# Attention scores over 64 rows: matmuls of the two row halves issued next to each other, in differential attention and in MLA

## The chip, the cores and the metric

One core of one Trainium2 chip runs the whole program, two transformer blocks of two layers each on 256 tokens of width 1024, in one launch. The metric is the device time of a launch in microseconds; a kernel's time is the median of its runs. Three runs of the kernel before gave 1356.26, 1359.81 and 1360.58 us.

## The reference

What is computed, cut to the two attentions that the change touches. Everything is float32.

```python
# first block, both layers: differential attention, 4 heads of two components of 64 each
s = jnp.einsum('bqhcd,bkhcd->bhcqk', qblk, k)      # c: component, contraction over 64
pr = jax.nn.softmax(s, axis=-1)
a = pr[:, :, 0] - lam * pr[:, :, 1]
o = jnp.einsum('bhqk,bkhe->bqhe', a, v)

# second block, layer 1: MLA, 8 heads; 128 "nope" dimensions and 64 with rotary positions
q = jnp.concatenate([q[..., :128], rope(q[..., 128:], positions)], axis=-1)
k = jnp.concatenate([k[..., :128], rope(k[..., 128:], positions)], axis=-1)
sc = jnp.einsum('bqhd,bkhd->bhqk', qi, k) * 192 ** -0.5     # causal mask on sc
o = jnp.einsum('bhqk,bkhd->bqhd', jax.nn.softmax(sc, axis=-1), v)
```

Around them stand a long convolution, a pooling mixer, projections and, in each of the four layers, a mixture of experts, whose weights make up nearly all of the 397 MB that the kernel reads.

## The kernel before

Weights come from HBM in tiles of 1 MB through one queue of SyncE (line 566). They land in a ring of 22 slots that they share with most intermediate tiles (`s8`); a transfer is issued when a slot is free, and a few tiles ahead of use. A projection splits each weight into a high and a low part (ScalarE line 593, VectorE line 595) and runs three matmuls per product. All matmuls are recorded at line 603 (`mm`) and all transposes by TensorE at line 616, so they are told apart by their tiles. A float32 matmul of `mm` shows as two MATMUL instructions with a weight load each; the bfloat16 mask shows as one.

The kernel is written against a tile framework. The source gives the order in which the instructions are made; when the program is built, a scheduler lays down each engine's queue, taking an instruction up when its operands and its buffer should be ready and preferring the one that comes earlier in the source. Each engine then works through its queue. PSUM has four banks under the name `pa` (`self.ps()`) and four under `pp` (`self.pp()`); a bank is given out again when its last reader is done.

**Differential attention** (`DiffAttention.scores`, line 319 on; called by `mix1` for two tiles of 128 queries, `qt`, and two pairs of heads, `hp`). `qkT` holds component 0 of a head in partitions 0 to 63 and component 1 in partitions 64 to 127. One call makes four score matmuls with a contraction over 64 rows, each 256 columns wide: two heads `z` of component `c` = 0 into bank `sc[0]`, then two of `c` = 1 into `sc[1]`. Behind each component come one row maximum (line 330) and two exponentials (line 333). `mix1` calls scores(0, 0) and scores(0, 1), then the projection of the values, and then interleaves `values`, scores(1, 0) and scores(1, 1); the output projection follows.

**MLA** (`mla`, with the inner functions `scores` and `values`). A call of `scores(hp)` handles two heads of one parity, heads 4·quad + par and 4·quad + par + 2, for both tiles `t` of 128 queries; keys run to (t + 1)·128. Per tile and head it makes three matmuls into one bank per tile: the causal mask (`identb`, `causb`), the nope part over 128 rows (`qnT`, `knT`), and the rope part over 64 rows (`qrT`, `krT`, both cut from the tile `RT`). Two heads of the same parity have their rope rows in the same half of the partitions. Then, per tile: one row maximum for both heads (line 1843), a multiply with the query scale (line 1844), two exponentials (line 1847), a reciprocal (line 1848) and two scalings (line 1850). `values(hp)` transposes the probabilities (tile `LX`), copies them (line 1863) and multiplies with `vv`. The order in the source is scores(0), scores(1), the projection of the values (`vup`), then values(0), scores(2), values(1), scores(3), values(2), values(3), and the attention to the memory (tiles `kv`, `MQ`).

Of the kernel before, what the change touches and what calls it, by code (L numbers as in the profile page):

```python
# [16 lines left out]
AF = mybir.ActivationFunctionType  # L17
OP = mybir.AluOpType
AX = mybir.AxisListType.X
# [274 lines left out]
def a2(a):  # L294
    return a.rearrange("p (a b) -> p a b", a=2)
# [6 lines left out]
def a8(a):  # L302
    return a.rearrange("p (a b) -> p a b", a=8)
# [6 lines left out]
class DiffAttention:  # L310
# [9 lines left out]
    def scores(self, qt, hp):  # L320
        k, nc, v = self.k, self.k.nc, self.k.nc.vector
        qs = slice(qt * 128, (qt + 1) * 128)
        sc = [k.ps(), k.ps()]
        ex, sm, cf = self.EX[:, hp], self.sm[qt], self.cf[qt]
        nm = k.sb([128, 2, 2], "anm", bufs=4)
        for c in range(2):
            for z in range(2):
                h = 2 * hp + z
                k.mm(sc[c][:, z * 256:(z + 1) * 256], self.qkT[c * 64:(c + 1) * 64, 0, h, qs], self.qkT[c * 64:(c + 1) * 64, 1, h, :], z == 0)
            v.tensor_reduce(nm[:, c, :], a2(sc[c]), axis=AX, op=OP.max, negate=True)  # L330
            for z in range(2):
                h = 2 * hp + z
                nc.scalar.activation(ex[:, z, c, :], sc[c][:, z * 256:(z + 1) * 256], AF.Exp, bias=nm[:, c, z:z + 1], accum_out=sm[:, c, h:h + 1])
        hs = slice(2 * hp, 2 * hp + 2)
        v.reciprocal(cf[:, 0, hs], sm[:, 1, hs])
        v.scalar_tensor_tensor(cf[:, 0, hs], cf[:, 0, hs], self.nlam, sm[:, 0, hs], op0=OP.mult, op1=OP.mult)
        for z in range(2):
            h = 2 * hp + z
            v.scalar_tensor_tensor(ex[:, z, 0, :], ex[:, z, 1, :], cf[:, 0, h:h + 1], ex[:, z, 0, :], op0=OP.mult, op1=OP.add)
# [130 lines left out]
class Kern:  # L470
# [1251 lines left out]
    def mla(self, hT, cat, row):  # L1722
        nc, v = self.nc, self.nc.vector
# [26 lines left out]
        knT = self.s8([128, 8, 256], "knT")  # L1750
        RT = self.s8([128, 2, 4, 256], "RT")
        qrT, krT = RT[:, 0], RT[:, 1]
# [27 lines left out]
        qs = self.sb([128, 3, 2, 8], "qss")  # L1780
        qnT = self.s8([128, 8, 256], "qnT")
# [23 lines left out]
        for t in range(2):  # L1805
# [3 lines left out]
            x, y = a8(pp[t]), a8(qx)  # L1809
            self.rotate((y[:, :, 0:32], y[:, :, 32:64]), (x[:, :, 0:32], x[:, :, 32:64]), [tq[:, t, j, :] for j in range(4)], [128, 8, 32])  # L1810
            p = self.ps()
# [5 lines left out]
        for t in range(2):  # L1817
# [3 lines left out]
            p = self.ps()  # L1821
# [5 lines left out]
        LX = self.s8([128, 2, 1024], "LX")  # L1827
        ex = {}

        def scores(hp):  # L1830
            par, quad = hp % 2, hp // 2
            for t in range(2):
                w = (t + 1) * 128
                ts = slice(t * 128, (t + 1) * 128)
                p = self.ps()
                for z in range(2):
                    h = 4 * quad + par + 2 * z
                    self.mm(p[:, z * w + t * 128:(z + 1) * w], self.identb, self.causb, z == 0)
                    self.mm(p[:, z * w:(z + 1) * w], qnT[:, h, ts], knT[:, h, 0:w], False)
                    self.mm(p[:, z * w:(z + 1) * w], qrT[par * 64:(par + 1) * 64, h // 2, ts], krT[par * 64:(par + 1) * 64, h // 2, 0:w], False)  # L1840
                r = qs[:, 2, t, 4 * quad + par:4 * quad + par + 3:2]
                nm = self.sb([128, 3, 2], "lnm", bufs=4)
                v.tensor_reduce(nm[:, 0, :], a2(p[:, :2 * w]), axis=AX, op=OP.max, negate=True)
                v.tensor_mul(nm[:, 0, :], nm[:, 0, :], r)
                e = a2(LX[:, hp % 2, t * 256:t * 256 + 2 * w])
                for z in range(2):
                    nc.scalar.activation(e[:, z, :], p[:, z * w:(z + 1) * w], AF.Exp, bias=nm[:, 0, z:z + 1], scale=r[:, z:z + 1], accum_out=nm[:, 1, z:z + 1])
                v.reciprocal(nm[:, 2, :], nm[:, 1, :])
                for z in range(2):
                    v.tensor_scalar(e[:, z, :], e[:, z, :], nm[:, 2, z:z + 1], None, op0=OP.mult)  # L1850
                ex[hp, t] = e

        def values(hp):
            par, quad = hp % 2, hp // 2
            po = self.pp()
            for z in range(2):
                h = 4 * quad + par + 2 * z
                pt = self.ps()
                self.transp(pt[:, 0:128], ex[hp, 0][:, z, :])
                self.transp(pt[:, 128:256], ex[hp, 1][:, z, 0:128])  # L1860
                self.transp(pt[:, 256:384], ex[hp, 1][:, z, 128:256])
                pT = self.tmp(384)
                nc.scalar.activation(pT, pt[:, 0:384], AF.Copy)
                self.mm(po[:, z * 256:(z + 1) * 256], vv[:, 0, h * 128:(h + 1) * 128], pT[:, 0:256], z == 0)
                self.mm(po[:, z * 256 + 128:(z + 1) * 256], vv[:, 1, h * 128:(h + 1) * 128], pT[:, 256:384], False)
            self.split(a2(po), cat.t[quad][0][:, par::2, :], cat.t[quad][1][:, par::2, :])

        scores(0)
        scores(1)
        for n in range(2):  # L1870
            pz = up2("vup", n)
            for t in range(2):
                nc.scalar.activation(vv[:, t, n * 512:(n + 1) * 512], pz[t], AF.Copy)
        for hp in range(4):
            values(hp)
            if hp < 2:
                scores(hp + 2)
# [192 lines left out]
```

## Time and profile before

| what | value |
|---|---|
| median of the three runs | 1359.81 us |
| the profiled execution's own time | 1360.22 us |
| its span, first to last instruction | 1358.6 us |
| TensorE matmul busy (PE) | 1233.9 us, 91% |
| weight load (PEld), VectorE (DVE), ScalarE (ACT) busy | 755.3, 644.7, 485.0 us |
| GpSimd (POOL) busy | 48.9 us |
| mean granted TensorE clock | 0.963 |
| read from HBM | 395.74 MB, 292 GB/s over the span |

All times below are microseconds from the start of the span. Matmuls are pipelined: their recorded durations overlap, so the cost of one is read from the distance between starts. PE counts as busy from the first start to the modelled end of such a row; a change in what the engine needs between two matmuls shows as distance, not always as idle time.

### The profile page before, as it was taken

Reading aid. Unit: us, or ns where it says so; the run is one execution under the profiler, and the core shown is the slowest. Engines: PE = TensorE matmul, PEld = TensorE weight load, DVE = VectorE, ACT = ScalarE, POOL = GpSimd, SP = SyncE. Lnnn points to the kernel's source line nnn. Section 1 sums busy time; section 2 is a strip of 40 time slices with the busy share of each in tenths; the row PEclk is TensorE's granted clock in tenths of the full one; section 3 lists DMA queues with packets and bytes.
Section 4 is the critical chain, followed back from the end, with each engine's and each line's share of the span. In section 5 each row is a group of like instructions: output and inputs, shape, how many; then the busy total and the mean of one; then the engine's idle time right before and its main releaser. Section 6 shows DMA issues by size and latency. Waiting matters only on the chain. (4 is left out here: it accounts for less than half of the span.)

```text
span 1358.6 us, 18043 instructions
## 1 busy us (share of the span) xinstructions
PE 1233.9 (91%) x6632; PEld 755.3 (56%) x6632; DVE 644.7 (47%) x1820; ACT 485.0 (36%) x991; POOL 48.9 (4%) x61
## 2 busy tenths in 40 slices
PE   6999999998999999998999888786899998977877
PEld 5777754456877764445888432231498676313222
DVE  6867853327868971216776410110387656101011
ACT  4456532224565642114665210010357653100001
POOL 1300000000200000000011000000000101000000
PEclk9999989998999999998999899899899998989989
DMA  9455568994154558997073899999960537999997
GB/s 373 182 220 208 186 259 344 422 415 184 66 217 178 228 216 368 400 402 308 29 278 145 326 408 421 421 421 422 393 246 31 223 119 301 422 421 421 421 422 253
DMA packets 68434, 398.07 MB, mean 293 GB/s; under 512 B 7408, under 2 KB 17904, under 8 KB 23024
## 3 DMA queue, kind: packets, MB, share of 16 engines
q1 hardware_dynamic: 68336, 396.82, 73.0%
q8 instruction: 55, 0.90, 0.3%
q14 instruction: 43, 0.35, 0.1%
HBM read 395.74 MB, written 1.05 MB: 292 GB/s over the span
## 5 line engine op out<-in xcount | busy, mean ns | idle before, releaser
L603 PE MATMUL pa<-w,xg 128*32 128x512 f32 (+1 forms) x1536 | 293.5, 651 | 52.8 <-DMA w<-in_w 52.2
L603 PEld LDWEIGHTS pa<-w,xg 128*32 128x32 f32 (+1 forms) x1536 | 78.6, 127 | 240.8 <-issue 137.0
L595 DVE TENSOR_TENSOR wlo<-w,whi 128x512 fp32r<-128x512 f32 (+1 forms) x260 | 178.3, 697 | 46.9 <-PE pp L603 36.6
L593 ACT ACTIVATE whi<-w 128x512 fp32r<-128x512 f32 (+1 forms) x260 | 158.0, 628 | 112.2 <-PE pp L603 93.5
L603 PE MATMUL pa<-w,tmp 128*32 128x512 f32 (+2 forms) x832 | 170.2, 575 | 13.3 <-DMA w<-in_w 13.1
L1321 DVE SCALAR_TENSOR_TENSOR tmp<-tmp,rgs,pa 128x256 f32<-128x256 f32 x32 | 15.4, 481 | 316.9 <-ACT tmp L1320 316.6
L613 DVE TENSOR_TENSOR wlo<-pa,whi 128x512 fp32r<-128x512 f32 (+1 forms) x68 | 44.9, 660 | 188.7 <-ACT whi L612 188.7
L603 PEld LDWEIGHTS pa<-w,tmp 128*32 128x32 f32 (+1 forms) x832 | 43.1, 119 | 100.9 <-issue 66.4
L612 ACT ACTIVATE whi<-pa 128x512 fp32r<-128x512 f32 (+1 forms) x68 | 38.9, 572 | 168.8 <-PE pa L603 168.8
L603 PE MATMUL pp<-wlo,hTh 128*128 128x512 f32 (+1 forms) x224 | 87.8, 395 | 1.9 <-DVE wlo L595 1.9
L603 PE MATMUL pp<-whi,hTh 128*128 128x512 f32 (+1 forms) x224 | 88.7, 396 | 0.0
L603 PE MATMUL pp<-whi,hTl 128*128 128x512 f32 (+1 forms) x224 | 87.9, 393 | 0.0
L603 PE MATMUL pp<-hTh,whi 128*128 128x256 f32 x256 | 75.1, 293 | 2.4 <-DVE hTh L895 2.4
L603 PE MATMUL pp<-hTh,wlo 128*128 128x256 f32 x256 | 74.4, 291 | 1.8 <-DVE wlo L595 1.7
L603 PE MATMUL pp<-hTl,whi 128*128 128x256 f32 x256 | 73.6, 288 | 0.0
L603 PE MATMUL pa<-rD,th 128*128 128x256 f32 x256 | 68.2, 303 | 1.3 <-DVE row L698 0.8
L1320 ACT ACTIVATE tmp<-pa,rgs 128x256 f32<-128x256 f32 x16 | 7.6, 473 | 166.1 <-PE pa L603 166.0
L603 PE MATMUL pa<-rD,tl 128*128 128x256 f32 x256 | 65.6, 293 | 0.0
L603 PEld LDWEIGHTS pa<-rD,th 128*128 128x128 f32 x256 | 51.5, 201 | 16.2 <-issue 12.4
L603 PEld LDWEIGHTS pp<-hTh,whi 128*128 128x128 f32 x256 | 50.7, 198 | 4.3 <-ACT whi L593 3.4
L603 PEld LDWEIGHTS pa<-rD,tl 128*128 128x128 f32 x256 | 51.7, 202 | 0.9 <-issue 0.8
L603 PEld LDWEIGHTS pp<-hTh,wlo 128*128 128x128 f32 x256 | 50.7, 198 | 2.5 <-DVE wlo L595 2.4
(456 smaller groups left out, 1990.1 us busy)
## 6 DMA issues: line engine op xcount, KB each, us to landing
w<-in_w SPq DMA_DIRECT2D x349, 1024.0 KB, 12.8
w<-in_w SPq DMA_DIRECT2D x32, 256.0 KB, 6.0
gb<-in_row SPq DMA_DIRECT2D x5, 1024.0 KB, 9.3
w<-in_w SPq DMA_DIRECT2D x8, 512.0 KB, 12.7
FI<-in_c SPq DMA_DIRECT2D x4, 512.0 KB, 8.0
w<-in_w SPq DMA_DIRECT2D x2, 640.0 KB, 10.6
h<-in_x SPq DMA_DIRECT2D x2, 512.0 KB, 4.2
PB<-in_row SPq DMA_DIRECT2D x2, 512.0 KB, 4.1
```

Source lines behind the costliest of these rows:

```text
L593: self.nc.scalar.activation(hi, w[:, c0:c0 + c], AF.Copy)
L595: self.nc.vector.tensor_sub(lo, w[:, c0:c0 + c], hi.bitcast(F32))
L603: self.last = self.nc.tensor.matmul(out, lhsT, rhs, start=start, stop=True, skip_group_check=True)
L612: self.nc.scalar.activation(hi, x, AF.Copy)
L613: self.nc.vector.tensor_sub(lo, x, hi.bitcast(F32))
L1320: nc.scalar.activation(a, pg[:, 0:256], AF.Silu, scale=1.0 if r["row"] is None else r["factor"][:, j:j + 1])
L1321: v.scalar_tensor_tensor(a, a, r["gate"][:, j:j + 1], pg[:, 256:512], op0=OP.mult, op1=OP.mult)
```

## The change

In `DiffAttention.scores` the loops over component and head change places for the matmuls: first both components of head 0, then both of head 1, so that neighbours lie in different halves of the rows. The maxima and exponentials come after all four matmuls.

In MLA a call now handles heads 2·hp and 2·hp + 1, whose rope rows lie in different halves. A bank belongs to a head and holds both query tiles. All masks and nope matmuls of the call come first, then the four rope matmuls with the two heads taking turns. The maxima become four per call, one for each head and tile; one multiply and one reciprocal serve the whole call; the reciprocal waits for all four exponentials. `values` and the placing in `cat` follow the new heads. The arithmetic stays the same.

```diff
-        for c in range(2):
-            for z in range(2):
+        for z in range(2):
+            for c in range(2):
                 h = 2 * hp + z
                 k.mm(sc[c][:, z * 256:(z + 1) * 256], self.qkT[...], self.qkT[...], z == 0)
+        for c in range(2):
             v.tensor_reduce(nm[:, c, :], a2(sc[c]), axis=AX, op=OP.max, negate=True)
...
         def scores(hp):
-            par, quad = hp % 2, hp // 2
+            ps = [self.ps(), self.ps()]
+            at = lambda t: slice(t * 128, 128 + t * 256)
+            for z in range(2):
+                for t in range(2):
+                    self.mm(ps[z][:, 256 * t:256 * t + 128], self.identb, self.causb, t == 0)
+                for t in range(2):
+                    self.mm(ps[z][:, at(t)], qnT[:, 2 * hp + z, ...], knT[:, 2 * hp + z, ...], False)
+            for t in range(2):
+                for z in range(2):
+                    zs = slice(z * 64, (z + 1) * 64)
+                    self.mm(ps[z][:, at(t)], qrT[zs, hp, ...], krT[zs, hp, ...], False)
+            nm = self.sb([128, 3, 2, 2], "lnm", bufs=2)
+            for z in range(2):
+                for t in range(2):
+                    v.tensor_reduce(nm[:, 0, t, z:z + 1], ps[z][:, at(t)], axis=AX, op=OP.max, negate=True)
+            v.tensor_mul(nm[:, 0], nm[:, 0], r)
             for t in range(2):
...
-                    self.mm(p[:, z * w + t * 128:(z + 1) * w], self.identb, self.causb, z == 0)
-                    self.mm(p[:, z * w:(z + 1) * w], qnT[:, h, ts], knT[:, h, 0:w], False)
-                    self.mm(p[:, z * w:(z + 1) * w], qrT[par * 64:(par + 1) * 64, ...], krT[...], False)
-                nm = self.sb([128, 3, 2], "lnm", bufs=4)
-                v.tensor_reduce(nm[:, 0, :], a2(p[:, :2 * w]), axis=AX, op=OP.max, negate=True)
-                v.tensor_mul(nm[:, 0, :], nm[:, 0, :], r)
...
+                    nc.scalar.activation(e[:, z, :], ps[z][:, at(t)], AF.Exp, bias=..., scale=..., accum_out=...)
+            v.reciprocal(nm[:, 2], nm[:, 1])
...
-            self.split(a2(po), cat.t[quad][0][:, par::2, :], cat.t[quad][1][:, par::2, :])
+            self.split(a2(po), cat.hir(2 * hp, 2 * hp + 2), cat.lor(2 * hp, 2 * hp + 2))
```

## Rows read from the trace of the kernel before

**Rows 1.** The page: busy time of each engine, share of the span, instructions.

```profile
PE 1233.9 (91%) x6632; PEld 755.3 (56%) x6632; DVE 644.7 (47%) x1820; ACT 485.0 (36%) x991; POOL 48.9 (4%) x61
```

**Rows 2.** The chain that ended last: start, length, what.

```profile
1151.99 5.60 PE pa L603 x48
...
1173.30 19.81 DMA w<-in_w
...
1332.57 1.57 PE pa L603 x2
```

**Rows 3.** By stretch: busy PE, PEld, DVE, ACT, POOL; clock; DMA share, GB/s.

```profile
107.50:114.40 6.90, 6.90 (x37) 4.87 (x35) 3.71 (x8) 4.50 (x16) 0.00 (x0) 1.00 0.40 152
1051.90:1060.50 8.60, 8.60 (x43) 4.95 (x41) 4.56 (x19) 6.25 (x17) 0.00 (x0) 1.00 0.68 249
1060.50:1081.10 20.60, 20.23 (x109) 14.56 (x109) 12.74 (x36) 12.76 (x36) 2.71 (x2) 1.00 0.41 144
1081.10:1120.00 38.90, 38.84 (x176) 30.71 (x175) 22.23 (x46) 22.38 (x48) 1.28 (x1) 1.00 0.41 158
...
190.00:200.00 10.00, 9.25 (x44) 5.54 (x45) 0.86 (x3) 3.11 (x6) 0.00 (x0) 0.66 1.02 426
```

**Rows 4.** Timeline of PE, first layer: start, length, instruction, count.

```profile
89.78 3.62 PE L603 MATMUL pa<-FI,VY 128*128 128x256 f32 x16
...
93.76 1.13 PE L603 MATMUL pa<-qkT 64*128 64x256 f32 x6
...
95.45 2.15 PE L603 MATMUL pa<-qkT 64*128 64x256 f32 x10
...
107.58 1.13 PE L603 MATMUL pa<-qkT 64*128 64x256 f32 x4
108.64 0.94 PE L603 MATMUL pa<-VY,AT 128*128 128x128 f32 x6
```

**Rows 5.** Score matmuls and weight loads of tile qkT alive in two short stretches.

```profile
93.76:93.78 0.02, 0.02 (x2) 0.02 (x2) 0.00 (x0) 1.00 0.00 0
107.58:107.88 0.30, 0.30 (x1) 0.29 (x2) 0.00 (x0) 1.00 0.00 0
```

**Rows 6.** Timeline of PE in MLA, scores(0), and the first transposes behind.

```profile
1052.80 0.23 PE L603 MATMUL pa<-causb,identb 128*128 128x128 bf16 x1
1052.87 0.44 PE L603 MATMUL pa<-knT,qnT 128*128 128x128 f32 x2
1053.23 0.49 PE L603 MATMUL pa<-RT 64*128 64x128 f32 x2
1053.65 0.23 PE L603 MATMUL pa<-causb,identb 128*128 128x128 bf16 x1
...
1054.93 0.23 PE L603 MATMUL pa<-causb,identb 128*128 128x128 bf16 x1
...
1062.42 1.09 PE L616 MATMUL pa<-ident,LX 128*128 128x128 f32 x6
```

**Rows 7.** Timeline of DVE, then ACT, in MLA: the softmax of the first pair.

```profile
1053.76 0.42 DVE L1843 TENSOR_REDUCE lnm<-pa 128x2 f32<-128x256 f32 x1 [0.56 <-PE pa L603]
1055.14 0.16 DVE L1844 TENSOR_TENSOR lnm<-lnm,qss 128x2 f32<-128x2 f32 x1
1056.31 0.69 DVE L1843 TENSOR_REDUCE lnm<-pa 128x2 f32<-128x512 f32 x1 [1.01 <-PE pa L603]
1058.75 0.48 DVE L1850 TENSOR_SCALAR LX<-LX,lnm 128x128 f32<-128x128 f32 x2
1064.53 0.62 DVE L1850 TENSOR_SCALAR LX<-LX,lnm 128x256 f32<-128x256 f32 x2
1055.38 1.28 ACT L1847 ACT_TABLE_LOAD   x1 [2.04 <-DVE lnm L1844]
1056.67 0.46 ACT L1847 ACTIVATE LX<-pa,lnm,qss 128x128 f32<-128x128 f32 x1
1058.73 0.46 ACT L1847 ACTIVATE LX<-pa,lnm,qss 128x128 f32<-128x128 f32 x1
```

More of the change, by code (lines that the diff above doesn't have):

```diff
@@ L1830, in scores @@
         def scores(hp):
-            par, quad = hp % 2, hp // 2
+            ps = [self.ps(), self.ps()]
[4 more added lines that the diff above has]
+                for t in range(2):
+                    self.mm(ps[z][:, at(t)], qnT[:, 2 * hp + z, t * 128:(t + 1) * 128], knT[:, 2 * hp + z, 0:(t + 1) * 128], False)
+            for t in range(2):
+                for z in range(2):
+                    zs = slice(z * 64, (z + 1) * 64)
+                    self.mm(ps[z][:, at(t)], qrT[zs, hp, t * 128:(t + 1) * 128], krT[zs, hp, 0:(t + 1) * 128], False)
@@ L1832, in scores @@
+            r = qs[:, 2, :, 2 * hp:2 * hp + 2]
+            nm = self.sb([128, 3, 2, 2], "lnm", bufs=2)
[3 more added lines that the diff above has]
+            v.tensor_mul(nm[:, 0], nm[:, 0], r)
             for t in range(2):
                 w = (t + 1) * 128
-                ts = slice(t * 128, (t + 1) * 128)
-                p = self.ps()
+                e = ex[hp, t] = a2(LX[:, hp % 2, t * 256:t * 256 + 2 * w])
@@ L1836, in scores @@
                 for z in range(2):
-                    h = 4 * quad + par + 2 * z
-                    self.mm(p[:, z * w + t * 128:(z + 1) * w], self.identb, self.causb, z == 0)
-                    self.mm(p[:, z * w:(z + 1) * w], qnT[:, h, ts], knT[:, h, 0:w], False)
-                    self.mm(p[:, z * w:(z + 1) * w], qrT[par * 64:(par + 1) * 64, h // 2, ts], krT[par * 64:(par + 1) * 64, h // 2, 0:w], False)
-                r = qs[:, 2, t, 4 * quad + par:4 * quad + par + 3:2]
-                nm = self.sb([128, 3, 2], "lnm", bufs=4)
@@ L1843, in scores @@
-                v.tensor_reduce(nm[:, 0, :], a2(p[:, :2 * w]), axis=AX, op=OP.max, negate=True)
-                v.tensor_mul(nm[:, 0, :], nm[:, 0, :], r)
-                e = a2(LX[:, hp % 2, t * 256:t * 256 + 2 * w])
-                for z in range(2):
[L1847 to L1850, printed above, removed]
@@ L1851, in scores @@
-                ex[hp, t] = e
+                    nc.scalar.activation(e[:, z, :], ps[z][:, at(t)], AF.Exp, bias=nm[:, 0, t, z:z + 1], scale=r[:, t, z:z + 1], accum_out=nm[:, 1, t, z:z + 1])
+            v.reciprocal(nm[:, 2], nm[:, 1])
+            for t in range(2):
+                for z in range(2):
+                    x = ex[hp, t][:, z, :]
+                    v.tensor_scalar(x, x, nm[:, 2, t, z:z + 1], None, op0=OP.mult)
         def values(hp):
-            par, quad = hp % 2, hp // 2
@@ L1855, in values @@
             po = self.pp()
             for z in range(2):
-                h = 4 * quad + par + 2 * z
+                h = 2 * hp + z
                 pt = self.ps()
```

## Prediction

> **What bounds the kernel now.** I read the page first: PE is busy for 91% of the span, the weight loads for 56%, every other engine for less [rows 1]. A share over the whole span doesn't tell what a change in one stage is worth, so I went to the chain that ended last. From 1158 us to 1332 us it is one weight transfer behind the other, and this stream was released by matmuls of the last experts' gather, 1151.99 to 1157.59 [rows 2]. Nothing ahead of that point is a transfer of the chain: whoever makes PE reach 1157 us earlier lets the stream start, and end, earlier. The third view is busy time by stretch [rows 3]: PE has no idle time in the first block's attention (6.90 of 6.90 us) and in the first part of MLA's scores (8.60 of 8.60), and hardly any behind (20.23 of 20.60, and 38.84 of 38.90 in the output projection). So both places of the change are bound by PE's queue, and what PE saves there should reach the end one for one, unless the softmax behind the scores can't follow. DVE and ACT have room: 12.7 us each of 20.6 [rows 3].
>
> **What a score matmul costs now.** In the timeline [rows 4] a run of four 64-row MATMULs (one component, two heads) starts at 107.58 and the next work at 108.64: 1.06 us. Float32 matmuls of the same width over 128 rows take (3.62 − 0.38) / 15 = 0.216 us from start to start [rows 4], where 0.38 is the length of the last one. Four would take 0.86 us, so 0.2 us of the run is the change to 64 rows. There are four such runs in each layer, where the source has two calls of eight: the queue was not laid down in the order of the source, since `values` came between the components.
>
> The first two calls show something else. Their run at 93.76 holds six MATMULs and takes the same 1.13 us as a run of four [rows 4]. In its first 20 ns two matmuls and two weight loads are alive [rows 5], while in the first 0.3 us of the run at 107.58 only one matmul is. By the source the run of six can only be head 0 and head 1 of component 0 and one head of component 1: matmuls of the two halves ran at the same time. So the overlap is real in this program, it costs no speed, and the first two calls have part of it already. What brings it is that both halves stand in one unbroken run of 64-row work.
>
> Here a rule of the Trainium skill can be weighed, "TensorE: Matmul & The Clock Gate", Part 3 (The mechanism): it says that matmuls start and end strictly in program order. By it the two instructions of one matmul would stay one behind the other, only the seam between neighbours would overlap, and a run of eight would take five steps and not four; over twelve runs that would be some 2 us less gain than below. The trace doesn't agree: two started within 20 ns and the six took the time of four.
>
> **First block, part by part.** Nothing is added but order. Calls (0, 0) and (0, 1) now take runs of 1.13 and 2.15 us [rows 4], 3.2 us with three of four pairs sharing. At best they become two runs of 1.06, a gain of about 1.1 us; but the break in the middle stays (other work of higher rank, and the fifth bank needed before one of the four `pa` banks is given back), so I take 0.2. Calls (1, 0) and (1, 1) take four runs, 4.24 us. Unbroken they would be two runs of 1.06, a gain of 2.1. If each is broken into two halves of one head each, a run is 2 × 0.22 + 0.2 = 0.64 us and the gain 4.24 − 2.56 = 1.7; if one matmul stands alone and three follow, 4.24 − 2 × (0.64 + 1.06) = 0.8. I take 1.5. The later maximum of component 0 (0.69 us of DVE per bank of 512 columns, [rows 7]) lies beside the output projection's matmuls, which follow in PE's queue; without that cover it would cost 0.69 us per call. Per layer 1.7, **3.4 us** for both; bounds 0 (the queue breaks every call) and 6.4.
>
> **MLA, the matmuls.** In scores(0) a tile of 128 keys and one head takes 1052.80 to 1053.65, 0.85 us, and with 256 keys 0.64 us on average, twice: (1054.93 − 1053.65) = 1.28 us per head [rows 6]. The mask is 0.07 us [rows 6]; by 0.216 us for 256 columns and half of it for 128, nope and rope together are 0.43 and 0.86. What is left, 0.35 us each time, is the change to 64 rows and back, paid for every rope matmul. A call is 2 × (0.85 + 1.28) = 4.26 us, with four changes. After: four masks 0.28, nope 0.65 × 2 = 1.30, one change 0.35, rope 0.65 if the halves overlap and 1.30 if not: 2.58 or 3.23. The gain is 1.7 or 1.0 per call, 6.8 or 4.1 us for four. By rows 5 I take the overlap: **−6.8 us**.
>
> **MLA, the softmax behind.** Before, the first tile's maximum started while PE worked on the second. Now all four wait for the last rope matmul. From the last score to the last scaled probability it was 0.69 + 0.16 + 2 exponentials + 0.16 + 0.62; four exponentials take 1058.73 − 1056.67 = 2.06 us [rows 7], the two wide ones 1.1, so 2.7 us. After: maxima of 256 columns 0.42 and of 128 some 0.29 (half the step from 0.42 to 0.69 less; an estimate), 1.42 in all, then 0.16 + 2.06 + 0.16 + 0.48 + 0.62: 4.9 us. That is 2.2 us more per call. Where it hides: in the middle calls behind `values` and the next scores. Where it doesn't: at the start, for the query scale is ready only at 1055.14 whatever PE does, and a table load of 1.28 us follows it [rows 7]. scores(0) would end at 1054.5; maxima to 1056.0, multiply and load to 1057.5, exponentials to 1059.5, scalings to 1060.7, against 1062.42 for the first transposes before [rows 6]: 1.7 us of the 3.4 us that two calls gained are left, so 1.7 are given back. At the end the last pair's 2.2 us stand against about 1 us of memory attention that can fill in: 1.2 more. I take **+2.9 us**; bounds 0 (a better order hides it) and 4 × 2.2 = 8.8. Bank `ps[0]` is also held until the third exponential and both through the call; that is in the rivals. DMAs: the calls issue none, and SyncE's and GpSimd's queues are not moved past. `lnm` goes from four small to two full buffers, the same four tiles of scores in flight, nothing. The other placing in `cat` costs the same instructions, nothing.
>
> **The sum.** −3.4 − 6.8 + 2.9 = −7.3 us. On the profiled execution, 1360.22 us (span 1358.6 and 1.6 around it), that is 1352.9; it ran 0.4 us above the median, so against the median **1352.5 us**. The clock adds noise either way: it was granted at full rate in both places but at 0.66 from 190 to 200 us [rows 3], behind a pause of PE, and a shift of the work by microseconds can move such stretches by 2 us in either direction. The likeliest case's own range is 1348 to 1356.
>
> **Rivals.** *The runs are broken or don't overlap.* The scheduler takes up what it thinks ready; other matmuls may go between the rope matmuls as they went between the components at 108.64 [rows 4]. Then only the saved changes of mode are left, 4.1 less some 1.5 of softmax in MLA and about 0.8 in the first block: −3.4, 1356.4 us. For it: the four broken runs. Against it: scores(0) and scores(1) lie unbroken for 8.6 us. *The softmax chain takes PE's place* (the slower side). Each call now holds two of four `pa` banks from its first mask to its last exponential, 2.6 + 1.4 + 0.2 + 2.1 = 6.3 us, and `values` wants two as well. If a call can't start before the one before has released its banks, the calls stand in a row: 4 × (2.6 + 4.9 + 2.4 for transposes, copies and values) = 39.6 us where 1051.9 to 1081.1, less 5 us of other projections, had 24: +15 less what fills, say half, and −3.4: 1364 us. It decides from the point where the next scores start behind the last exponentials of the call before. Against it: the bank time of a call, 2 × 6.3 + 2 × 2 for the transposes, is 4.1 us on four banks, under the 5.0 us of PE work per call. In a sentence by itself: the Trainium skill, "TensorEngine Tiling (Array Packing)", Performance Considerations (PSUM Bottleneck), says that array tiling speeds the matmuls and not the emptying of PSUM, which is this rival; no row here shows it yet. *It doesn't reach the end*: something ahead of 1157 us that is no matmul holds the time, such as the router's chain on DVE; 1359.8. Against it: that chain itself waits for PE's output projection.
>
> **Chances.** Forecast 0.58, broken runs 0.22, softmax chain 0.12, doesn't reach the end 0.08. A measurement can tell some 0.3% (4.1 us) from no change: faster is under 1355.7, slower over 1363.9. Nearly all of the forecast's case and a fourth of the broken runs lie under it, 0.61; the chain gives 0.09 above and the rest is the same, 0.30. The range reaches to no change on one side and on the other to the first block's and MLA's better bounds in part (−13): 1346.5 to 1361.
>
> **What would show it.** In the changed profile: runs of eight score MATMULs in about 1.1 us, or two of four in 0.64; per MLA call four rope matmuls in 1.0 us and the call in 2.6; the first `LX` transposes near 1060 less the first block's 3.4; the start of the last weight stream earlier by the whole gain. Wrong: PE idle before `LX` transposes for more than 3 us in all, PE's queue with other matmuls inside the calls, or a PE distance of 0.2 us between rope matmuls of different halves.

## The result, and the profile after

Five runs of each kernel on one chip gave 1367.73 us (1366.95 to 1368.75) after the change and 1360.58 us (1356.26 to 1363.34) before it. The ratio is 1.0053, with a 95% interval of 1.0038 to 1.0069: 7 us slower, where 1352.5 us and a gain of 7.3 us were predicted. The measured time lies outside the range.

The page of after: busy time, share of the span (1367.1 us), instructions. TensorE has 7 us less work than in [rows 1] and the span is 8.5 us longer.

```profile
PE 1226.8 (90%) x6632; PEld 751.0 (55%) x6632; DVE 642.4 (47%) x1820; ACT 485.1 (35%) x991; POOL 48.7 (4%) x61
```

The chain that ended last, of after, where it leaves TensorE (start, length, what). The last weight stream is still released by 48 matmuls of the gather, but these now take 8.90 us against 5.60 [rows 2], and the second transfer of the stream behind them starts at 1180.23 us and not at 1173.30.

```profile
1158.93 8.90 PE pa L604 x48
...
1180.23 19.82 DMA w<-in_w
```

To see where the time went I cut the span at instructions that all the kernels have, and took their starts from the timeline of TensorE: layer 0 and layer 1 of the first block from the first score matmul (93.76 before, [rows 4]) to the first expert matmul (tiles `w`, `xg`); MLA from the twelve transposes of `W` just ahead of scores(0) (1050.58 before) to the first matmul of `MP` and `kv` in the memory attention behind (1089.98); the router from there to the second 32 expert matmuls behind the gather (1157.77 before); and the rest to the end of the span.

| kernel (one profiled execution each) | layer 0 | layer 1 | MLA | router | rest |
|---|---|---|---|---|---|
| before | 86.12 | 117.68 | 39.41 | 67.79 | 200.86 |
| before_again | 86.08 | 117.73 | 39.41 | 67.83 | 199.36 |
| after | 90.79 | 122.76 | 37.73 | 71.80 | 199.14 |
| block_alone | 89.57 | 121.22 | 39.42 | 67.90 | 199.61 |
| one_call | 91.14 | 121.20 | 39.42 | 67.83 | 199.66 |
| block_gate | 86.10 | 119.19 | 40.98 | 67.62 | 199.66 |
| mla_alone | 86.09 | 119.23 | 37.72 | 71.76 | 198.53 |
| mla_again | 86.09 | 119.25 | 40.99 | 70.67 | 197.63 |
| mla_third | 86.12 | 117.73 | 39.31 | 66.94 | 201.22 |
| same_half | 86.11 | 117.70 | 39.49 | 67.72 | 201.20 |
| rope_runs | 86.11 | 117.73 | 37.75 | 71.80 | 197.51 |
| no_rope | 86.10 | 117.73 | 35.81 | 67.90 | 199.00 |
| per_tile | 86.09 | 119.19 | 38.69 | 68.73 | 199.79 |
| tile_first | 86.11 | 117.72 | 42.08 | 68.64 | 197.45 |
| after_gate | 86.07 | 119.20 | 37.73 | 71.76 | 198.25 |
| residual_dve | 86.11 | 119.29 | 37.38 | 66.74 | 199.39 |
| best | 86.10 | 119.24 | 37.37 | 66.73 | 199.61 |
| before_residual | 86.11 | 119.23 | 41.19 | 67.49 | 199.06 |

How to read it: steps of 1.5 to 1.8 us in layer 1 and MLA come and go in kernels that run the same code there (mla_alone, mla_again and mla_third are one kernel, and MLA takes 37.72, 40.99 and 39.31 us in them); they are short stretches at half clock (in layer 1 of mla_alone the granted clock is 0.91 from 494 to 512 us, in before 1.00; in MLA of mla_third it is 0.50 from 1060 to 1063 us). So two MLA stretches are alike only where the clock is the same in both. MLA is free of such a fall in before, before_again, after, block_alone, one_call, mla_alone, same_half, rope_runs, after_gate, residual_dve and best; it has one in the other kernels, and two in mla_again. What stands out of the steps: after loses 4.7 us in layer 0 and 5.1 in layer 1 (3.5 without such a step), gains 1.7 in MLA, and loses 4.0 at the router, where nothing was changed. What lies outside the five stretches varies too: in block_alone it is 3.5 us shorter than in before, so that its profiled run (1362.64 us) is the fastest of its six.

**The first block.** TensorE in layer 0 of after: start, length, instruction, count, in brackets the idle time before and who ended it.

```profile
92.03 1.13 PE L604 MATMUL pa<-qkT 64*128 64x256 f32 x6
105.87 0.70 PE L604 MATMUL pa<-qkT 64*128 64x256 f32 x4
107.36 0.70 PE L604 MATMUL pa<-qkT 64*128 64x256 f32 x4
109.90 1.61 PE L604 MATMUL pa<-qkT 64*128 64x256 f32 x6
112.52 0.70 PE L604 MATMUL pa<-qkT 64*128 64x256 f32 x2
124.78 0.63 PE L617 MATMUL pa<-ident,AT 128*128 128x128 f32 x4 [1.57 <-DVE AT L372]
134.57 1.99 PE L604 MATMUL pp<-w,PB 128*128 128x512 f32 x4 [0.48 <-DVE h L1432]
```

Call (1, 0) takes two runs of 0.70 us where it took two of 1.13 [rows 4]. Call (1, 1) is broken otherwise than before, with `c` = 1 of head 1 by itself, and saves nothing. The 1.57 us are new: TensorE waits for the multiply into `AT` that ends `norm(0)`. Over the whole layer TensorE is without work for 3.0 us, in before for 0.3. On DVE, that chain runs from a row sum to the multiply, first of before, then of after (with two of the instructions between them):

```profile
115.06 0.68 DVE L364 TENSOR_REDUCE acf<-AT 128x4 f32<-128x512 f32 x1
...
121.67 0.69 DVE L371 TENSOR_TENSOR AT<-pa,acf 128x512 f32<-128x512 f32 x1
```

```profile
113.86 0.68 DVE L365 TENSOR_REDUCE acf<-AT 128x4 f32<-128x512 f32 x1
...
122.67 0.69 DVE L596 TENSOR_TENSOR wt<-w,wt 128x512 fp32r<-128x512 f32 x1
123.28 0.16 DVE L371 SCALAR_TENSOR_TENSOR acf<-acf 128x4 f32<-128x4 f32 x1
...
123.95 0.68 DVE L372 TENSOR_TENSOR AT<-pa,acf 128x512 f32<-128x512 f32 x1
```

Counted from the layer's first score matmul (93.76 and 92.03) it starts 0.5 us later and its multiply 4.0 us later: 10.1 us from start to start where it took 6.6. Between its ends stand eleven weight splits of 0.6 to 0.7 us where there were four; six of the eleven are splits for the tail of the output projection (`wt`), which in before came behind the multiply. Behind this, the clock falls as well: by stretch (length, then busy PE, PEld, DVE, ACT, POOL, granted clock, DMA share, GB/s) after has 2.8 us at 0.50, the lower level of 1.2 GHz, where before has full clock from 150 to 156 us. block_alone has full clock there too, and loses 3.5 us in layer 0: that is the part without the clock.

```profile
153.50:156.30 2.80, 2.80 (x10) 2.41 (x10) 0.67 (x3) 1.60 (x4) 0.00 (x0) 0.50 0.00 0
```

**MLA.** The same view of TensorE, in after:

```profile
1061.55 0.93 PE L604 MATMUL pa<-RT 64*128 64x128 f32 x8
1062.40 0.28 PE L604 MATMUL pa<-causb,identb 128*128 128x128 bf16 x2
...
1068.86 1.07 PE L617 MATMUL pa<-ident,LX 128*128 128x128 f32 x6 [1.72 <-DVE LX L1859]
...
1076.01 0.27 PE L604 MATMUL pa<-causb,identb 128*128 128x128 bf16 x2 [1.41 <-ACT LX L1854]
...
1084.20 0.50 PE L617 MATMUL pa<-ident,LX 128*128 128x128 f32 x2 [1.49 <-DVE LX L1859]
```

Four ropes stand in one row of 0.93 us, the next work starts after 0.85; the call from 1059.81 to 1062.40 takes 2.59 us against 4.26 [rows 6]. But TensorE now waits three times (and 0.31 us a fourth time, as in before): for the scaled probabilities of the first pair, for a bank that exponentials still read, and for the last pair's probabilities. Over the whole MLA stretch (columns as above) before has 0.4 us without a busy TensorE, after 5.0 us:

```profile
1050.58:1089.98 39.40, 38.98 (x199) 27.29 (x200) 24.78 (x73) 26.61 (x70) 3.99 (x3) 1.00 0.56 214
```

```profile
1058.47:1096.20 37.73, 32.74 (x200) 24.73 (x200) 24.09 (x73) 26.23 (x70) 3.85 (x3) 1.00 0.57 224
```

The work shrank by 6.2 us, the stretch by 1.7.

**The router.** Behind the gather, the first 32 expert matmuls of after take 6.23 us, the next 32 3.64 as in before; from 1158.5 to 1167.7 the granted clock is 0.63.

```profile
1161.47 6.23 PE L604 MATMUL pa<-w,xg 128*32 128x512 f32 x32
1168.00 3.64 PE L604 MATMUL pa<-w,xg 128*32 128x512 f32 x32
```

```profile
1158.50:1167.70 9.20, 9.20 (x53) 4.31 (x54) 1.13 (x5) 3.06 (x5) 0.00 (x0) 0.63 1.01 424
```

### The profile page after: what moved, and what is told of

It is laid out like the page before. It is cut to its first block, busy times and chain, and to the rows that moved or that the text cites. A ratio compares the mean times of both kernels' runs of the same rounds, so it can differ in the third digit from the quotient of the medians.

```text
span 1367.1 us, 18053 instructions
## 1 busy us (share of the span) xinstructions
PE 1226.8 (90%) x6632; PEld 751.0 (55%) x6632; DVE 642.4 (47%) x1820; ACT 485.1 (35%) x991; POOL 48.7 (4%) x61
```

## Experiments

Ratios are to the kernel before on the same chip, with the 95% interval. Where a kernel had one run, its profile is what counts.

**Which half of the change loses.** *mla_alone* has the MLA of after and the first block of before; *block_alone* the other way round.

> MLA changed, first block as before. Theory (all of the loss lies in the first block, where the row statistics of differential attention are finished later): the MLA stretch gains what the two traces showed there, 1.7 us, so 1.5 to 2.5 us faster than before, about 1358. Rival (the longer softmax chain of MLA is the loss): 3 us slower or more. If the two parts disturb each other through the clock, neither number holds.

> First block changed, MLA as before. Theory: layer 0 loses 4.7 us between 100 and 160 us and layer 1 3.6 us between 390 and 440, with PE idle 1.5 us ahead of the transposes of AT in each layer: 7 to 9 us slower than before, about 1368. Rival (the first block gains the forecast 1 to 3 us and the loss comes from elsewhere): 1357 to 1360.

mla_alone: 1360.85 us against 1359.75, ratio 1.0010 (0.9998 to 1.0022). block_alone: 1367.29, ratio 1.0067 (1.0048 to 1.0086). So the loss is the first block's, as expected. But MLA gives nothing that the runs can tell from no change, though its stretch is shorter by the 1.7 us in this profile; the router takes 4.0 us more. (The profiled run, 1363.18 us, is the slowest of the twelve.)

**What tips the first block.** *one_call* keeps before's order in three of the four calls.

```diff
+        if (qt, hp) == (1, 0):
+            order = [(0, 0), (1, 0), (0, 1), (1, 1), "r0", "r1"]
+        else:
+            order = [(0, 0), (0, 1), "r0", (1, 0), (1, 1), "r1"]
```

> MLA as before; in the first block only call (1, 0) takes the new order of its four score matmuls, the three other calls stay as before. Theory (the saving in this call lets ScalarE and PE come to the tail's splits earlier, and the order on DVE tips there): the whole loss of the first block, 7 to 9 us slower than before, though only a quarter of the block's change is made. Rival (each of the calls loses its share): 2 us slower.

1368.00 us, ratio 1.0072 (1.0049 to 1.0096). One call of four carries the whole loss, with the same 1.57 us ahead of `AT`. Which part of it moves the scheduler isn't separated: in this call the matmuls take less time, and the maximum of component 0 comes later.

```profile
126.26 0.63 PE L627 MATMUL pa<-ident,AT 128*128 128x128 f32 x4 [1.57 <-DVE AT L382]
```

**Whether DVE's order is the cause.** *block_gate* is block_alone with the tail's splits laid behind the end of `norm(0)` on DVE, and nothing else moved by hand.

```diff
+        k.normed[qt] = v.tensor_mul(on, p4, cf[:, 3, :, None].to_broadcast([128, 4, 128]))
...
         held = []
+        if name.startswith("wout"):
+            self.hold(self.normed[0])
         for i in range(n_ - tail, n_):
```

> First block changed, MLA as before, and in addition the eight weight splits of the tail of the output projection are held back on DVE until the multiply that ends norm(0) (into AT). The same instructions, another order on DVE only. Theory (these splits between the small steps of norm(0) delay it, and PE waits for it): the idle time of 1.5 us ahead of the transposes of AT is gone, the chain from the first reduce to AT takes 7 us and not 10, and the loss of 8 us goes with it; 0 to 2 us faster than before, 1358 to 1360. Rival (the loss comes from the score matmuls themselves, from later maxima or held banks): still 6 us or more slower than before.

1361.47 us, ratio 1.0015 (1.0002 to 1.0028): 5.8 of the 7.5 us are back. TensorE's timeline has no idle time of note ahead of `AT`, and the chain on DVE takes 7.2 us (116.07 to 123.28):

```profile
124.12 0.63 PE L618 MATMUL pa<-ident,AT 128*128 128x128 f32 x4
```

```profile
116.07 0.68 DVE L365 TENSOR_REDUCE acf<-AT 128x4 f32<-128x512 f32 x1
...
123.28 0.69 DVE L372 TENSOR_TENSOR AT<-pa,acf 128x512 f32<-128x512 f32 x1
123.89 1.89 DVE L597 TENSOR_TENSOR wt<-w,wt 128x512 fp32r<-128x512 f32 x3
```

Layer 0 takes 86.10 us, as in before: the loss is gone, and the 0.85 us saved in call (1, 0) don't come through either, even now. Over the layer TensorE is busy 0.4 us less than in before and without work 0.4 us more, most of it in a longer wait for `norm(1)` (0.17 us in before):

```profile
134.86 0.66 PE L618 MATMUL pa<-ident,AT 128*128 128x128 f32 x4 [0.42 <-DVE AT L372]
```

So the score matmuls alone don't set the time there; that `norm` does is the likely reading, and no run takes its wait out. A rival is left for a small part: the ratio's interval lies just above 1.

**Whether the overlap is real, and what it needs.** *same_half* lets a call take two heads of one parity again and keeps the rest of MLA's change; *rope_runs* keeps the heads and issues head 0's two ropes ahead of head 1's.

```diff
-            for t in range(2):
-                for z in range(2):
+            for z in range(2):
+                for t in range(2):
                     zs = slice(z * 64, (z + 1) * 64)
```

> First block as before. MLA as changed, except that a call again takes two heads of one parity, so that its four rope matmuls lie in the same half of the rows and can't run at the same time; what is left of the change is the order (one change to 64 rows per call instead of four) and the softmax for the whole call. If the overlap is real, the four ropes take 1.5 to 1.6 us instead of 0.93 and a call 3.2 instead of 2.6. Theory (PE waits for the softmax in any case): the stretch of MLA is less than 1.5 us longer than with the whole change. Rival (PE's queue still sets the time): 2.6 us longer.

> First block as before. MLA as changed, but the four rope matmuls of a call stand in the order head 0 tile 0, head 0 tile 1, head 1 tile 0, head 1 tile 1: only the two in the middle are neighbours from different halves. Theory (the halves run each through its own share of the queue, as a third matmul in the queue was seen to start with the first): head 1 tile 0 starts with or shortly after head 0 tile 0, the four take 0.93 to 1.0 us as with the change. Rival (matmuls start strictly in the order of the queue and only neighbours overlap): 1.2 us or more.

The four ropes of scores(0), in same_half and in rope_runs:

```profile
1054.06 1.57 PE L603 MATMUL pa<-RT 64*128 64x128 f32 x8
```

```profile
1054.84 0.93 PE L603 MATMUL pa<-RT 64*128 64x128 f32 x8
```

The overlap is worth 0.64 us per call. It doesn't need neighbours: counting tile `RT` alone, two MATMULs run in the first 20 ns of rope_runs (busy PE counts x2), though by the source both ropes of head 0 come first. That they aren't the two of one matmul is seen in same_half, where the first runs by itself.

```profile
1054.84:1054.86 0.02, 0.02 (x2) 0.02 (x2) 0.00 (x0) 1.00 0.00 0
```

```profile
1054.06:1054.08 0.02, 0.02 (x1) 0.02 (x1) 0.00 (x0) 1.00 1.77 410
```

same_half has 2.6 us more TensorE work than mla_alone, and its MLA stretch is 1.8 us longer (39.49), between the two expectations, and as long as before's (39.41): without the overlap, MLA's stretch gains nothing from the new order. Its one run gave 1360.98 us, as mla_alone; that of rope_runs 1360.44.

**Whether TensorE still sets MLA's time.** *no_rope* leaves out the sixteen rope matmuls of mla_alone.

> First block as before, MLA as changed; the sixteen rope matmuls are left out, so that TensorE has 3.7 us less to do (four times 0.93) and nothing else changes. Theory (in the changed kernel TensorE no longer sets the time of MLA's stretch, the softmax chain does): the stretch shortens by less than 1.5 us more than with the change, PE's idle time grows by the rest. Rival (TensorE still sets it): 3.7 us shorter.

Its one run gave 1356.72 us. The stretch takes 35.81 us, 1.9 shorter than in mla_alone, of 3.7 us of work. But its clock is 0.50 from 1061.7 to 1065 us (the six transposes behind the longer wait took 1.51 us where mla_alone has 1.07), and that of mla_alone is full. The like case is mla_third, at 0.50 for as long and behind the same transposes: against its 39.31 us the stretch is 3.5 us shorter. So nearly all of what TensorE saves comes through, close to the rival. It doesn't part the two quite: the maxima of a call wait for its last rope, so leaving the ropes out also starts the softmax earlier.

```profile
1061.75 1.51 PE L616 MATMUL pa<-ident,LX 128*128 128x128 f32 x6 [2.67 <-DVE LX L1854]
```

**Whether a shorter softmax gives MLA's gain back.** *per_tile* does multiply, exponentials, reciprocal and scalings per query tile again; *tile_first* orders the matmuls by tile too, masks, nope and ropes of tile 0 first.

> First block as before. MLA: the matmuls of the change (two heads from different halves, ropes next to each other), but multiply, exponentials, reciprocal and scalings per query tile again. Theory (what MLA gives back, 4.9 us of PE idle time in the changed kernel, is the softmax chain made longer by waiting for all four maxima and all four exponentials): the first exponential starts 0.5 us earlier after the scores, the last scaling comes 1 us earlier, the first transposes of LX come 1 us earlier, and the stretch of MLA gains 3 to 4 us on before instead of 1.7. Rival (PE waits for banks held by the scores, not for the chain): the stretch gains 1.7 as with the change.

> First block as before. MLA as in the experiment per_tile, and the matmuls also tile by tile: masks, nope and the two ropes of query tile 0, then those of tile 1. It costs one change to 64 rows more per call (0.35 us, 1.4 us over four calls) and lets the softmax of tile 0 start beside the matmuls of tile 1, as before. Theory (chain): a call takes 2.9 us instead of 2.6, the idle time of PE falls from 4.9 us to about 2, the stretch of MLA gains 3 to 5 us on before. Rival (banks): the idle time stays and the stretch gains 0.5 or less.

per_tile: 1360.28 us, ratio 1.0010 (1.0000 to 1.0020). tile_first: 1363.30 us, 1.0029 (1.0019 to 1.0040). Both are misses. The MLA stretch of per_tile is 38.69 us, 1.0 longer than in mla_alone; but it too has a fall of the clock (0.50 from 1064.1 to 1067.4 us), and against mla_third it is 0.6 us shorter, less than half of the 1.3 to 2.3 that the theory expected beyond the change. Its first pair waits longer, and in pieces:

```profile
1062.29 0.33 PE L616 MATMUL pa<-ident,LX 128*128 128x128 f32 x1 [2.28 <-ACT LX L1852]
```

ACT and DVE show why: the exponentials of tile 0 are ready early, three copies of `vv` follow, and then those of tile 1 still wait 1.64 us for their multiply. On DVE this multiply takes 1.21 us, and the two scalings of tile 0 ahead of it 1.48 where a later pair of the same shape takes 0.47, while two subtractions run on GpSimd.

```profile
1058.31 1.64 ACT L1876 ACTIVATE vv<-pp 128x512 f32<-128x512 f32 x3
1061.59 0.56 ACT L1852 ACTIVATE LX<-pa,lnm,qss 128x256 f32<-128x256 f32 x1 [1.64 <-DVE lnm L1848]
```

```profile
1058.94 1.48 DVE L1855 TENSOR_SCALAR LX<-LX,lnm 128x128 f32<-128x128 f32 x2
1060.34 1.21 DVE L1848 TENSOR_TENSOR lnm<-lnm,qss 128x2 f32<-128x2 f32 x1
...
1064.28 0.47 DVE L1855 TENSOR_SCALAR LX<-LX,lnm 128x128 f32<-128x128 f32 x2
```

```profile
1058.85 2.68 POOL L651 TENSOR_TENSOR wlo<-h,whi 128x512 fp32r<-128x512 f32 x2 [9.30 <-DVE lnm L1853]
```

So it isn't the length of the chain alone; what runs beside its links counts as much. per_tile without GpSimd beside it wasn't run, so what a shorter chain is worth stays open. tile_first's idle time didn't fall either (2.05 us ahead of the first transposes), and 1.2 us more went at half clock ahead of its first call (the twelve transposes of `W` in 2.66 us, not 1.50).

**GpSimd beside the scalings.** In after, DVE's multiply takes 1.00 us and the first four scalings 1.88; the next four, of the same shapes, take 1.01. GpSimd runs two subtractions of the residual from 1065.97 to 1068.63.

```profile
1063.69 0.16 DVE L1849 TENSOR_TENSOR lnm<-lnm,qss 128x4 f32<-128x4 f32 x1
...
1066.30 1.00 DVE L1849 TENSOR_TENSOR lnm<-lnm,qss 128x4 f32<-128x4 f32 x1
...
1067.56 1.88 DVE L1859 TENSOR_SCALAR LX<-LX,lnm 128x128 f32<-128x128 f32 x4
...
1069.72 1.01 DVE L1859 TENSOR_SCALAR LX<-LX,lnm 128x128 f32<-128x128 f32 x4
```

```profile
1065.97 2.66 POOL L652 TENSOR_TENSOR wlo<-h,whi 128x512 fp32r<-128x512 f32 x2 [9.28 <-PE pp L604]
```

The Trainium skill, "SBUF — State Buffer", section SBUF: two separate sides, says that the port pair which VectorE and GpSimd share is an exclusive lock held for a whole instruction. The trace agrees: the 0.16 us multiply ends at 1067.30, about where the first of the two subtractions must, if each takes half of the 2.66 us. *residual_dve* is mla_alone with these subtractions on VectorE; *before_residual* does the same to the kernel before.

```diff
-            y = self.residual(g)
+            y = self.residual(v if i == 1 else g)
```

> First block as before, MLA as changed; in the second block's layer 1 the four subtractions of the residual run on VectorE instead of GpSimd. Theory (the query scale's multiply took 1.00 us and four scalings 1.89 us where the same four took 1.01 us a little later, because GpSimd's subtractions ran beside them): without them 0.2 and 1.0 us, the first transposes of LX come 0.5 to 1 us earlier, the stretch of MLA gains 2 to 2.5 us instead of 1.7, less what the four subtractions of 0.68 us cost on VectorE. Rival (the scalings take that long for themselves): no change ahead of LX, and the stretch gains less than 1.7.

> The kernel before, with the four subtractions of the residual in the second block's layer 1 on VectorE and nothing of the change. Theory (in the kernel before TensorE has no idle time in MLA's stretch, so GpSimd's share costs nothing there): as before within 1 us. Rival (what made residual_dve faster has nothing to do with the change of MLA): 1.5 to 2.5 us faster than before.

residual_dve: 1358.13 us against 1359.54, ratio 0.9985 (0.9972 to 0.9999), the only kernel whose whole interval lies below 1. The multiply takes 0.16 us and the scalings 1.00, the wait ahead of the first transposes falls from 1.72 to 1.32, and the stretch is 0.35 us shorter than mla_alone's; the larger part of the difference to mla_alone is at the router, 66.74 us, with no half clock on the expert matmuls. That the residual brings the latter isn't shown: mla_third, below, has 66.94 with the residual on GpSimd.

```profile
1062.92 1.00 DVE L1858 TENSOR_SCALAR LX<-LX,lnm 128x128 f32<-128x128 f32 x4
```

```profile
1063.35 1.07 PE L616 MATMUL pa<-ident,LX 128*128 128x128 f32 x6 [1.32 <-DVE LX L1858]
```

before_residual: 1360.28 us against 1359.89, ratio 1.0007 (0.9998 to 1.0016), so the step alone gains nothing without the changed MLA.

**Where MLA's gain went.** *mla_again* and *mla_third* are mla_alone, *before_again* is before, for a further profile each.

> The same kernel as mla_alone, to see whether the stretch at half clock behind the second block's router comes again. In its first profile the 32 expert matmuls that start at 1156.55 us took 6.21 us and not 3.64. Theory (the place where TensorE pauses has moved against the clock, so it belongs to this kernel): 6.2 us again, and the gain of MLA is lost there. Rival (it falls at random): 3.64 us in this execution.

> The kernel before once more, to see in a second profile whether its expert matmuls behind the second block's last router run at full clock again. If the half clock belongs to the changed MLA: 3.64 us for the first 32 expert matmuls behind the gather, as in the first profile. If it falls at random: 5 to 6 us are as likely here as in the changed kernels.

> The same kernel as mla_alone, a third execution. If the half clock behind the last router belongs to this kernel: 5 to 6.2 us for the 32 expert matmuls behind the gather, as twice before. If it falls at random: 3.64.

The first 32 expert matmuls behind the gather, in mla_alone, mla_again and mla_third:

```profile
1156.55 6.21 PE L603 MATMUL pa<-w,xg 128*32 128x512 f32 x32
```

```profile
1158.23 5.06 PE L603 MATMUL pa<-w,xg 128*32 128x512 f32 x32
```

```profile
1150.84 3.64 PE L603 MATMUL pa<-w,xg 128*32 128x512 f32 x32
```

before_again has 3.64 as before. One run each gave 1362.84 (mla_again), 1357.59 (mla_third) and 1359.94 us (before_again). The half clock there isn't fixed to the kernel, since one of three executions is free of it, and that one is the fastest; but with the MLA of after and the residual on GpSimd it stood in five of six profiles (after, mla_alone, mla_again, rope_runs, after_gate; not mla_third) and in none of the five of before (twice) or of the first block's change alone (block_alone, one_call, block_gate). Of the variants of MLA, tile_first has it (5.34 us), per_tile, same_half and no_rope don't. What decides it isn't settled. It accounts for the size: 4 us are lost at the router, 1.7 were gained in MLA, and the rest is 1.6 us shorter on the mean of those five profiles than of the five without it. Nor is the clock inside MLA the same as before: of the six profiles, mla_again and mla_third fall to half clock behind the new wait ahead of the first `LX` transposes, which costs some 1.6 us each time, and no profile with before's MLA falls at that place.

**Both remedies.** *after_gate* is after with the gate of block_gate; *best* adds the residual on VectorE.

> The whole change, with the eight weight splits of the output projection's tail held behind the multiply that ends norm(0), as in the experiment block_gate. Theory (order of DVE in the first block is the loss, MLA gives 1.7 us in its stretch and as much or more is lost behind it): 1360 to 1362, as the kernel before within 2 us, and 6 us faster than the change as it is. Rival (the two parts don't add up): 1365 or more.

> The whole change, with the tail's weight splits held behind norm(0) (as in after_gate) and the residual's four subtractions in the second block's layer 1 on VectorE (as in residual_dve). Theory (the two remedies add up, and without GpSimd beside it neither the scalings nor the stretch behind the router lose time): 1357 to 1359, 1 to 3 us faster than before. Rival (the first block's part still costs 1 us, and the rest is chance): 1359.5 to 1361.

after_gate: 1359.80 us against 1359.54, ratio 1.0002 (0.9988 to 1.0017). best: 1358.85 against 1359.89, 0.9988 (0.9975 to 1.0001). The parts add up: the gate takes back what the change lost, and best comes out 1.6 us below the kernel before by the ratio, with an interval that still touches no change.

## Why the prediction was wrong

- **What bounds the kernel.** That whoever lets TensorE reach the gather earlier moves the end was right: the gather's 48 matmuls still release the stream, though not one for one: in after they end 10.2 us later and the span is 8.5 longer. That TensorE's queue bounds the first block's attention because it has no idle time there was wrong. In block_gate TensorE does the scores in 0.85 us less and layer 0 takes as long as before.
- **First block, the runs.** The forecast was 1.7 us per layer, 1.5 of it from calls (1, ·) and 0.2 from calls (0, ·). The unbroken half runs came as forecast, 0.63 us from start to start against 0.64, but only in call (1, 0): 0.85 us. Call (1, 1) was broken in a way I hadn't priced, and calls (0, ·) kept a run of six.
- **First block, "costed at nothing".** This step turned the sign. "Nothing is added but order" was followed through on TensorE's queue only. I named the output projection's matmuls as the cover for a later maximum; the maximum isn't what cost the time. With the new order of call (1, 0) the scheduler brought the tail's weight splits forward on DVE, between the small dependent steps of `norm(0)`, and the cover, the same output projection, ended before `AT` was ready: 4.7 and 5.1 us in after instead of −1.7 per layer. one_call and block_gate show it from two sides; why the scheduler moved the splits was not tested.
- **MLA, the matmuls.** 2.59 us per call, against 2.58 forecast; ropes with overlap and one change of mode. Right, as was the reading of rows 5. The rule of the Trainium skill that the prediction weighed there ("TensorE: Matmul & The Clock Gate", Part 3, The mechanism: matmuls in program order) doesn't hold between the two halves: in rope_runs the first and, by the source, the third matmul were alive in the same 20 ns.
- **MLA, the softmax.** 2.9 us forecast as given back, 4.9 measured (1.72 + 1.41 + 0.31 + 1.49). The start was right: the first `LX` transposes were forecast at 1060.7 in the time of before and came at 1060.97 (1068.86 less the 7.89 us by which the stretch starts later); in part this is luck, since GpSimd's hold-up, 0.4 us by residual_dve, was not in the forecast. The end was 1.49 against 1.2. What was mis-sized is the middle, priced at nothing: there 1.41 us are a wait for a bank that is held until the third exponential (the 0.31 us beside it are also in before). That is the mechanism of the rival *the softmax chain takes PE's place*, at one of three places and not at all of them.
- **Behind MLA.** That MLA's gain reaches the end one for one was wrong in most of the profiled executions. I had put the clock at 2 us either way and at random; in the profiles with the changed MLA it went against it five times in six.
- **The sum.** Forecast −3.4 − 6.8 + 2.9; in the profile +4.7 + 5.1 in the first block, −1.7 in MLA and +4.0 at the router, less 1.7 in the rest and 1.9 outside the stretches: +8.5 us of span. The rivals were all about matmuls and softmax, and none had the order on DVE; slower had 0.09.

## What to carry to other kernels

When a scheduler lays the queues, a change of order on one engine is a change on all: look for the chain of small dependent steps on another engine whose end the next stage waits for, and ask what may now be laid between them. "No idle time" on an engine doesn't show that it is the bound; it can be filler that ends just as the chain behind is ready. Before counting on a gain in a stage, work out who is second, and remove that too: here the splits ahead of `norm`, and GpSimd beside the scalings. And before two stretches are compared, the granted clock in both has to be: without it, no_rope and per_tile read the other way.

## What the runs showed of the hardware

- Matmuls over different halves of the rows overlap whether or not they are neighbours in the queue. In rope_runs the third (by the source) and the first were alive together in the first 20 ns, and four ropes took 0.93 us in either order, 1.57 us in one half.
- A subtraction on GpSimd held up a multiply of four columns on VectorE for 1.00 us instead of 0.16, and four scalings for 1.88 instead of 1.01.
- Behind the same pause of 0.7 us on TensorE ahead of the gather, the same 32 matmuls of one kernel (mla_alone) took 6.21, 5.06 and 3.64 us in three executions: the granted clock over them (0.50 from 1157 to 1160 us in mla_alone, 1.00 from 1152 to 1155 in mla_third) can give or take more than MLA's gain.
